# The block inverse's doubling in four half slots instead of two slots, and attention's first row maxima and two of its slots ahead of the recurrence

## The chip, the cores and the metric

The kernel runs on one core of a Trainium2 chip. The metric is the device time of one launch in microseconds (us). Before the change the median of three runs is 3781.65 us (3773.04 to 3784.24). The profiled execution, which all rows below come from, took 3778.69 us.

## The reference

Two layers of a diffusion backbone work on 128 context tokens and 1024 latent tokens of width 1024. In each layer one input projection feeds three groups of heads: a bidirectional recurrence (RWKV-7, 4 heads of 64, two directions), attention over compressed keys (8 heads), and a gated chunk MLP. One output projection joins them, a normalisation follows, then a SwiGLU feed-forward part and a second normalisation. The two groups that matter here are these, cut to their core:

```python
# recurrence, for each direction, each head and each token
s_kk = einsum('hvk,hk->hv', S, -kk_t)
S = S * w_t[None] + s_kk[..., None] * (kk_t * a_t) + v_t[..., None] * k_t
y_t = einsum('hvk,hk->hv', S, r_t)
# attention, for each head and block of queries
s = q_nope @ k_nope.T + q_rope @ k_rope.T
o = softmax(s * MLA_SCALE) @ v
```

All arithmetic is fp32 in its result; the kernel makes an fp32 product of three products of rounded halves (lines L119 to L121, high by high, high by low, low by high).

## The kernel before, in words

The recurrence is computed in blocks of 64 tokens: within a block the tokens depend on each other through a triangular matrix, whose inverse is needed, and between blocks a state `S` is handed on. There are nine segments of 128 tokens (`segs`: the context, then eight of latent tokens), each with both directions. For a segment, `rw_operands` loads the columns `zin` and `szin` (L994, L996), multiplies them out into `AR` and `BK` (DVE L1032 to L1035, POOL L1031 and L1038, ACT L1016 to L1021), makes the triangular matrices `M1` on PE (L1052), and hands over to `rw_solve`. That routine writes the matrices to DRAM and reads back their 16 x 16 diagonal blocks `Db`, 64 of them, one in each partition. DVE inverts these blocks by doubling: from 1 x 1 to 2, 4, 8 and 16 (`for s in (2, 4, 8)` after a first copy, L1093). Each doubling is two products (`x` = 0 and 1), each of them some multiplications (L1113) and a sum (L1114). The result `Xb` goes, with its transpose (L1118), to DRAM as `xbd` (L1120) and comes back as `xz` in four loads (L1125), spread to the shape that PE wants. `rw_double` builds the 64 x 64 inverses from it on PE (L1140 to L1164), and `rw_scan` carries the state: `R` (L1182), `UV` (L1188 to L1191), the sums `St` and `S` on DVE (L1208, L1209), the outputs `Y`. For finished blocks of tokens `rw_post` normalises, gates and stores them in six steps (L1243 to L1279); its working tile `po_y` has two buffers.

Attention is a generator (`other`). For one head and 512 queries it computes the row maxima of a later unit (PE L735 with DVE L740 and L746, then through PE L753 and ACT L754 as one more row of the queries `qT`), the scores (L119 to L121), the exponentials (ACT L762, into `P` with four buffers), the sums over them (POOL L847), and the products with the values (PE L867). At a unit's end come the sums' reciprocal (DVE L777) and the store of the result (ACT's queue, L782). The next unit's keys, queries and values are loaded from ACT's queue as well (L786, L729, L791). One yield of the generator is half a group: two key tiles' scores with up to two row maxima, or the products of the group before.

In the stretch around the change the order of all five engines is written by hand (`manual_schedule`). A turn `i` of the loop has six slots; in slot `k` the function `slot(first, work)` emits attention's next half (scores and maxima), then the list `first`, then attention's other half (products, reciprocal), then the list `work`. The lists hold one step each of `rw_scan` of segment `i`, of `flow[i + 1]` to `flow[i + 3]` (the operands and solves of later segments) and of `rw_post`. Turn -2 is the first, so that segment 0's scan has its inverse; after the loop attention alone goes on with the last posts, and then the generator's rest up to the output projection, whose weights (`wr<-in_w_out_dram`, L309) and rows (`wr<-yd`, L1311) are loaded there. Engines run their own lists in order and wait for each other by semaphores; SP issues the loads and stores that the code puts on `nc.sync`.

Of the kernel before, what the change touches and what calls it, by code (L numbers as in the profile page):

```python
# [8 lines left out]
F32 = mybir.dt.float32  # L9
# [69 lines left out]
class Net:  # L79
# [637 lines left out]
    def mla(self, l, ap):  # L717
# [81 lines left out]
        q_tiles = {x: [self.t(ap, [NQR, 2, nq], f"qT{x}{i}", F32R) for i in range(n)] for x, nq, n in (("", 512, 3), ("c", 128, 2))}  # L799
        k_tiles = [self.t(ap, [NQR, 2, NK], f"kT{i}", F32R) for i in range(2)]  # L800
        for n, t in enumerate([k_tiles[0], q_tiles[""][0], q_tiles[""][1], q_tiles["c"][0], k_tiles[1], q_tiles[""][2], q_tiles["c"][1]]):
            (nc.gpsimd if n % 2 else nc.vector).memset(t[96:128].bitcast(F32), 0.0)
        for t in k_tiles:
            nc.vector.memset(t[96:97, 0].bitcast(F32), 1.0)
            nc.sync.dma_start(t[64:96].bitcast(F32), self.krd)

        units = [(h, q) for h in range(8) for q in ([0], [T_LAT, 512])]
# [82 lines left out]

    def rwkv(self, l, rp, other):
        nc = self.nc
        g2 = self.t(rp, [128, 256], "rg2")
        nc.gpsimd.dma_start(g2, self.I["rw_g2"][l])
        hv = self.t(rp, [128, 4], "rhv")
        nc.vector.tensor_scalar(hv[:, 0:2], self.v(l, "rw_ka", 0, 2), -1.0, None, op0=ALU.mult)
        nc.vector.tensor_scalar(hv[:, 2:4], self.v(l, "rw_ka", 0, 2), -1.0, 1.0, op0=ALU.mult, op1=ALU.add)

        brk = self.t(rp, [128, 2, 128], "brk")
        for ct in range(2):  # L900
            nc.vector.tensor_scalar(brk[:, ct], self.bones, self.v(l, "rw_rk", ct), None, op0=ALU.mult)

        Q = self.t(rp, [128, 8, 64], "Q")
        nc.gpsimd.memset(Q, 0.0)

        Xb = self.t(rp, [64, 2, 256], "Xb")
        nc.gpsimd.memset(Xb[:, 0], 0.0)
        nc.gpsimd.memset(Xb[:, 0, 0:256:17], 1.0)

        sl = self.t(rp, [64, 2, 4, 64], "so")  # L910
        for d in range(2):
            nc.gpsimd.dma_start(sl[:, d], self.I["state_rwkv"][0, l, d].rearrange("h v k -> v h k"))
        p = self.psum("rc")
        for ct in range(2):
            for d in range(2):
                nc.tensor.transpose(p[:, 64 * (2 * ct + d):64 * (2 * ct + d) + 64], sl[:, d, 2 * ct:2 * ct + 2].rearrange("p a b -> p (a b)"), self.ident[0:64, 0:64])
        S_lat = self.t(rp, [128, 2, 2, 64], "S", bufs=3)
        nc.vector.tensor_copy(S_lat.rearrange("p c u v -> p (c u v)"), p[:, 0:256])
        state = {True: None, False: S_lat}
        Y = self.t(rp, [128, NT, 2, 128], "Y")  # L920

        segs = [(T_LAT, 0, True)] + [(128 * i, T_CTX + 128 * i, False) for i in range(8)]
        n = len(segs)
        kept = [{} for _ in segs]
        flow = [self.rw_operands(segs[i], rp, hv, Q, Xb, self.xbd[i % 4], kept[i]) for i in range(n)]

        def turn(g):
            return lambda: next(g, None)  # L930

        def slot(first, work):

            next(other, None)
            for f in first:
                f()
            next(other, None)
            for f in work:
                f()
        def end_of_context():  # L940
            p = self.psum("rc")
            for d in range(2):
                for ct in range(2):
                    nc.tensor.transpose(p[0:64, 128 * (2 * d + ct):128 * (2 * d + ct) + 128], state[True][:, ct, d, :], self.ident)
            so = self.t(rp, [64, 512], "so")
            nc.vector.tensor_copy(so, p[0:64])
            nc.sync.dma_start(self.O["o_state"][0, l].rearrange("d h v k -> v (d h) k"), so.rearrange("p (a k) -> p a k", k=64))
        for _ in range(6):
            next(flow[0])
        next(other)  # L950

        E = mybir.EngineType
        with self.tc.manual_schedule(engines={E.PE, E.DVE, E.Activation, E.Pool, E.SP}):
            post, posts = [], []
            for i in range(-2, n):
                scan = self.rw_scan(segs[i], rp, Y, state, **kept[i]) if i >= 0 else iter(())
                ends = [turn(p) for p in posts]
                posts = [self.rw_post(l, b, rp, Y, g2, brk) for b in post]
                post = []
                for k in range(6):  # L960
                    first, work = [turn(p) for p in posts], [turn(scan)]
                    if 0 <= i + 2 < n:
                        work.append(turn(flow[i + 2]))
                    if 0 <= i + 3 < n:
                        (first if k == 2 else work).append(turn(flow[i + 3]))
                    if 0 <= i + 1 < n and k != 1:
                        (first if k > 1 else work).append(turn(flow[i + 1]))
                    if (i, k) == (1, 2):
                        first.insert(0, end_of_context)
                    slot(first, work + (ends if k == 0 else []))  # L970
                if i == 0:
                    post.append(8)
                if i >= 5:
                    post += [8 - i, i - 1]
            ends = [turn(p) for p in posts]
            posts = [self.rw_post(l, b, rp, Y, g2, brk) for b in post]
            for k in range(7):
                slot([], [turn(p) for p in posts] + (ends if k == 0 else []))
# [92 lines left out]
    def rw_solve(self, rp, M1, Xb, xd, kept):  # L1071

        nc = self.nc
        rows = (slice(0, 64), slice(64, 128))

        diag = lambda a: a.rearrange("g j (b r) -> (g j b) r", b=4)[:, 0:1024].rearrange("q (s t) -> q s t", t=64)[:, :, 0:16]
        full = lambda a: a[:, 0:4096].rearrange("j (s t) -> s j t", t=64)
        ltd = self.t(self.dram, [2, 8, 4160], "ltd", bufs=2)  # L1080
        for g in range(2):
            nc.sync.dma_start(full(ltd[g]), M1[rows[g], 1 - g, :, :, 0:64].rearrange("p c u t -> p (c u) t"))
        yield
        Db = self.t(rp, [64, 16, 16], "Db", bufs=2)
        nc.sync.dma_start(Db, diag(ltd))
        yield

        X, D = Xb[:, 0], Db.rearrange("p a b -> p (a b)")

        def at(a, o, *dims):  # L1090

            return bass.AP(a.tensor, a.offset + o, [a.ap[0], *([x, y] for x, y in dims)])
        nc.vector.tensor_copy(at(X, 16, (34, 8)), at(D, 1, (34, 8)))  # L1093
        for s in (2, 4, 8):
            b = 8 // s
            q = self.t(rp, [64, 64], "Xq")
            for x in range(2):
                pr = self.t(rp, [64, 512], "pr_x")

                if x == 0:  # L1100
                    l, m = (D, s, 34 * s, 1, 0, 16), (X, 0, 34 * s, 0, 1, 16)
                    o = q[:, 0:s * s * b]
                else:
                    l, m = (X, 17 * s, 34 * s, 16, 0, 1), (q, 0, s * s, 0, 1, s)
                    o = at(X, 16 * s, (34 * s, b), (16, s), (1, s))

                def part(a, o, sb, si, sj, sk):

                    if s == 2:
                        return [at(a, o + j * sj, (sb, b), (si, s), (sk, s)) for j in range(s)]  # L1110
                    return [at(a, o + i * sb, (si, s), (sj, s), (sk, s)) for i in range(b)]
                for p_, l_, m_ in zip(part(pr, 0, s ** 3, s * s, s, 1), part(*l), part(*m)):
                    nc.vector.tensor_tensor(p_, l_, m_, op=ALU.mult)  # L1113
                nc.vector.tensor_reduce(o, pr[:, 0:s ** 3 * b].rearrange("p (a k) -> p a k", k=s), axis=AX.X, op=ALU.add)  # L1114
            if s == 4:
                yield
        Xs, Xt = (Xb[:, x].rearrange("p (a b) -> p a b", a=16) for x in range(2))
        nc.vector.tensor_copy(Xt, Xs.rearrange("p a b -> p b a"))  # L1118
        for x, y in enumerate((Xs, Xt)):
            nc.sync.dma_start(diag(xd[x]), y)  # L1120
        yield
        xz = kept["xz"] = self.t(rp, [128, 2, 8, 64], "xz", bufs=3)
        for x in range(2):
            for g in range(2):
                nc.sync.dma_start(xz[rows[g], x], full(xd[x, g]))  # L1125
        yield
# [99 lines left out]
    def rw_post(self, l, b, rp, Y, g2, brk):  # L1226
# [13 lines left out]
        def tmp(tag):  # L1240
            return self.t(rp, [128, 2, 128], tag, bufs=2)
        p = bank()
        nc.tensor.matmul(p, self.bones, y, start=True, stop=True)  # L1243
        yc = tmp("po_y")
        nc.vector.scalar_tensor_tensor(yc, p, -1.0 / 64, y, op0=ALU.mult, op1=ALU.add)
        sq = tmp("po_t")
        nc.scalar.activation(sq, yc, AF.Square)
# [414 lines left out]
```

## Time and profile before

| | |
|---|---|
| median of three runs | 3781.65 us |
| profiled execution | 3778.69 us, its span 3776.9 us |
| mean granted TensorE clock | 0.957 of full speed |
| PE busy in the span | 3519.4 us (93%) |
| DVE, ACT, POOL busy | 1883.6 (50%), 1098.7 (29%), 1372.8 us (36%) |
| recurrence beside attention, layer 0 | 366 to 785 us |
| the same, layer 1 | 2236 to 2665 us |

The span is almost filled by PE, and what isn't lies for a good part in the two stretches of the last rows. A clock of 0.5 in a stretch is the lower of TensorE's two levels (1.2 GHz), 1.0 the higher (2.4 GHz).

### The profile page before, as it was taken

Reading aid. Unit: us, or ns where it says so; the run is one execution under the profiler, and the core shown is the slowest. Engines: PE = TensorE matmul, PEld = TensorE weight load, DVE = VectorE, ACT = ScalarE, POOL = GpSimd, SP = SyncE. Lnnn points to the kernel's source line nnn. Section 1 sums busy time; section 2 is a strip of 40 time slices with the busy share of each in tenths; the row PEclk is TensorE's granted clock in tenths of the full one; section 3 lists DMA queues with packets and bytes.
Section 4 is the critical chain, followed back from the end, with each engine's and each line's share of the span. In section 5 each row is a group of like instructions: output and inputs, shape, how many; then the busy total and the mean of one; then the engine's idle time right before and its main releaser. Section 6 shows DMA issues by size and latency. Waiting matters only on the chain.

```text
span 3776.9 us, 61399 instructions
## 1 busy us (share of the span) xinstructions
PE 3519.4 (93%) x25199; PEld 3048.4 (81%) x25199; DVE 1883.6 (50%) x3076; ACT 1098.7 (29%) x2156; POOL 1372.8 (36%) x1223
## 2 busy tenths in 40 slices
PE   8998788888999999999999988888998999999996
PEld 6888566666988888988988885666778999999995
DVE  3545665655733333333455465566559333333356
ACT  3443444423421111111144434343333311111111
POOL 2322656644511111111543237556445111111145
PEclk9999788999999999999999998899999999999998
DMA  7566545434332222221325565444343111111122
GB/s 288 158 220 164 114 100 104 96 77 149 107 107 78 90 79 78 67 67 56 107 103 143 192 147 109 99 97 88 78 159 107 51 45 45 39 40 45 45 84 78
DMA packets 466137, 387.13 MB, mean 102 GB/s; under 512 B 171148, under 2 KB 398856, under 8 KB 464640
## 3 DMA queue, kind: packets, MB, share of 16 engines
q1 hardware_dynamic: 372608, 249.12, 23.7%
q10 hardware_dynamic: 87424, 118.42, 10.4%
q0 software_dynamic: 5824, 15.66, 1.3%
q8 instruction: 198, 3.24, 0.4%
q14 instruction: 83, 0.68, 0.1%
HBM read 280.10 MB, written 103.02 MB: 101 GB/s over the span
## 4 chain that ended last, share of the span: by engine, by line
PE 74%; DVE 12%; DMA 6%; issue 2%; ACT 2%; POOL 1%; SPq 1%; ACTq 0%; POOLq 0%; DVEq 0%
PE b L119 19%; PE b L121 18%; PE b L120 18%; PE b L867 3%; DVE pr_x L1113 2%; PE b L355 2%; PE b L242 2%; DMA xz<-xbd 2%; DVE mx L740 1%; PE b L735 1%; PE b L406 1%; DVE hyl L126 1%; PE b L1140 1%; DMA zin<-zd 1%; DVE rc L777 1%
## 5 line engine op out<-in xcount | busy, mean ns | idle before, releaser
L121 PE MATMUL b<-hyh,w 128*128 128x384 f32 x2544 | 858.8, 338 | 1.4 <-DVE w L319 1.4
L119 PE MATMUL b<-hyh,w 128*128 128x384 f32 x2448 | 823.1, 336 | 0.0
L120 PE MATMUL b<-hyl,w 128*128 128x384 f32 x2448 | 821.9, 336 | 0.0
L319 POOL TENSOR_TENSOR w<-wr,w 128x2048 fp32r<-128x2048 f32 x64 | 296.9, 4640 | 1189.2 <-ACT w L316 989.0
L121 PEld LDWEIGHTS b<-hyh,w 128*128 128x128 f32 x2544 | 479.0, 188 | 26.3 <-issue 23.9
L119 PEld LDWEIGHTS b<-hyh,w 128*128 128x128 f32 x2448 | 460.1, 188 | 20.8 <-issue 19.4
L120 PEld LDWEIGHTS b<-hyl,w 128*128 128x128 f32 x2448 | 460.1, 188 | 9.7 <-issue 8.3
L1406 DVE TENSOR_TENSOR fs<-fs,b 128x384 f32<-128x384 f32 x132 | 72.9, 553 | 627.1 <-PE b L121 623.0
L847 POOL TENSOR_TENSOR acc<-acc,P 128x512 f32<-128x512 f32 x224 | 297.1, 1326 | 179.4 <-ACT P L762 169.9
L316 ACT CAST w<-wr 128x2048 fp32r<-128x2048 f32 (+2 forms) x86 | 161.2, 1874 | 583.8 <-PE b L120 511.9
L120 PE MATMUL b<-w,hidh 128*128 128x512 f32 x756 | 299.5, 396 | 0.0
L121 PE MATMUL b<-w,hidl 128*128 128x512 f32 x756 | 299.4, 396 | 0.0
L119 PE MATMUL b<-w,hidh 128*128 128x512 f32 x756 | 298.3, 396 | 0.0
L126 DVE TENSOR_TENSOR hidl<-fs,hidh 128x384 fp32r<-128x384 f32 x126 | 230.6, 1831 | 81.5 <-ACT hidh L125 79.5
L1420 DVE TENSOR_TENSOR acc<-acc,b 128x512 f32<-128x512 f32 x288 | 191.5, 684 | 139.0 <-PE b L121 139.0
L762 ACT ACTIVATE P<-b 128x512 f32<-128x512 f32 x288 | 169.7, 600 | 207.8 <-PE b L121 176.8
L740 DVE TENSOR_REDUCE mx<-b 128x1 f32<-128x512 f32 x256 | 169.0, 682 | 120.2 <-PE b L735 119.4
L867 PE MATMUL b<-P,vt 128*64 128x256 f32 x1152 | 180.1, 432 | 3.9 <-ACT P L762 3.2
L119 PE MATMUL b<-w,hyh 128*128 128x256 f32 x576 | 167.0, 292 | 16.9 <-ACT hyh L125 5.4
L125 ACT CAST hidh<-fs 128x384 fp32r<-128x384 f32 x126 | 64.4, 512 | 396.4 <-DVE fs L1406 396.4
L119 PE MATMUL b<-qT,kT 128*128 128x512 f32 x288 | 138.4, 480 | 38.3 <-DVE mx L740 30.0
L1405 ACT ACTIVATE fs<-b 128x384 f32<-128x384 f32 x132 | 64.8, 493 | 372.5 <-PE b L121 362.2
(437 smaller groups left out, 6953.1 us busy)
## 6 DMA issues: line engine op xcount, KB each, us to landing
wr<-in_ffn_w_in_dram SPq DMA_DIRECT2D x88, 512.0 KB, 4.7
fx<-in_ada_w_dram SPq DMA_DIRECT2D x28, 1024.0 KB, 5.1
wr<-in_ffn_w_out_dram SPq DMA_DIRECT2D x22, 1024.0 KB, 4.8
wr<-in_ada_w_dram SPq DMA_DIRECT2D x20, 1024.0 KB, 8.8
qT<-qd ACTq DMA_DIRECT2D x32, 448.0 KB, 6.3
zin<-zd SPq DMA_DIRECT2D x36, 384.0 KB, 5.3
xres<-x ACTq DMA_DIRECT2D x27, 512.0 KB, 3.6
wr<-in_w_in_dram SPq DMA_DIRECT2D x12, 1024.0 KB, 6.2
```

The source lines that it names most:

```text
L119: mm(out, ah, bh, start=(i == 0), stop=False)
L120: mm(out, ah, bl, start=False, stop=False)
L121: mm(out, al, bh, start=False, stop=(i == n - 1))
L126: (lo_eng or self.nc.vector).tensor_tensor(lo, src, hi.bitcast(F32), op=ALU.subtract)
L242: nc.tensor.matmul(p[32 * jj:32 * jj + 32, :], self.sc[:, 2 * jj + e, :], w[:, 2 * j + e, :], start=(e == 0), stop=(e == 1), tile_position ...
L316: self.nc.scalar.copy(hi, r)
L319: (eng or self.nc.gpsimd).tensor_tensor(lo[:, s], r[:, s], hi[:, s].bitcast(F32), op=ALU.subtract)
L740: nc.vector.tensor_reduce(mx[:, i, c:c + 1], p, axis=AX.X, op=ALU.max)
L762: nc.scalar.activation(P[:, 0:nq], p[:, 0:nq], AF.Exp, scale=MLA_SCALE)
L847: nc.gpsimd.tensor_tensor(acc, Ps[0] if k == 1 else acc, P, op=ALU.add)
L867: nc.tensor.matmul(po[0][64 * i:64 * i + 64, 0:256], vt[:, k], Ps[k][:, 256 * i:256 * i + 256], start=(k == 0), stop=(k == 9))
L1420: nc.vector.tensor_tensor(acc[i][:, w], acc[i][:, w], p, op=ALU.add)
```

## The change

- `kT`, `qT` and `qTc` are cleared, and the rows of ones set, by POOL alone; before, DVE made six of these nine fills.
- `rwkv` takes attention's first step, which is the first unit's row maxima (and the second unit's loads), as its first act, ahead of its own set-up (`rg2`, `hv`, `brk`, the states); before, that step came after the first six steps of `flow[0]`.
- Two slots with attention alone precede the loop's first turn.
- `rw_solve` yields after the second product of s = 2, after that of s = 4, after the first product of s = 8, and after the copy and the stores; before, it yielded after s = 4 and after the stores. So the doubling takes four half slots (`first` and `work` of slots 4 and 5) instead of the `work` of slots 4 and 5.
- The steps of `flow[i + 1]` go into `first` in every slot but slot 1; before, in slots 0 they stood in `work`. These steps include the four `xz` loads.
- `po_y` has four buffers instead of two.

```diff
@@ -799,9 +799,9 @@
         q_tiles = {x: [self.t(ap, [NQR, 2, nq], f"qT{x}{i}", F32R) for i in range(n)] for x, nq, n in (("", 512, 3), ("c", 128, 2))}
         k_tiles = [self.t(ap, [NQR, 2, NK], f"kT{i}", F32R) for i in range(2)]
         for n, t in enumerate([k_tiles[0], q_tiles[""][0], q_tiles[""][1], q_tiles["c"][0], k_tiles[1], q_tiles[""][2], q_tiles["c"][1]]):
-            (nc.gpsimd if n % 2 else nc.vector).memset(t[96:128].bitcast(F32), 0.0)
+            nc.gpsimd.memset(t[96:128].bitcast(F32), 0.0)
         for t in k_tiles:
-            nc.vector.memset(t[96:97, 0].bitcast(F32), 1.0)
+            nc.gpsimd.memset(t[96:97, 0].bitcast(F32), 1.0)
             nc.sync.dma_start(t[64:96].bitcast(F32), self.krd)
 
         units = [(h, q) for h in range(8) for q in ([0], [T_LAT, 512])]
@@ -890,6 +890,7 @@
 
     def rwkv(self, l, rp, other):
         nc = self.nc
+        next(other)
         g2 = self.t(rp, [128, 256], "rg2")
         nc.gpsimd.dma_start(g2, self.I["rw_g2"][l])
         hv = self.t(rp, [128, 4], "rhv")
@@ -947,11 +948,12 @@
             nc.sync.dma_start(self.O["o_state"][0, l].rearrange("d h v k -> v (d h) k"), so.rearrange("p (a k) -> p a k", k=64))
         for _ in range(6):
             next(flow[0])
-        next(other)
 
         E = mybir.EngineType
         with self.tc.manual_schedule(engines={E.PE, E.DVE, E.Activation, E.Pool, E.SP}):
             post, posts = [], []
+            for _ in range(2):
+                slot([], [])
             for i in range(-2, n):
                 scan = self.rw_scan(segs[i], rp, Y, state, **kept[i]) if i >= 0 else iter(())
                 ends = [turn(p) for p in posts]
@@ -960,11 +962,13 @@
                 for k in range(6):
                     first, work = [turn(p) for p in posts], [turn(scan)]
                     if 0 <= i + 2 < n:
-                        work.append(turn(flow[i + 2]))
+
+                        for part in (first, work) if k > 3 else (first if k == 3 else work,):
+                            part.append(turn(flow[i + 2]))
                     if 0 <= i + 3 < n:
                         (first if k == 2 else work).append(turn(flow[i + 3]))
                     if 0 <= i + 1 < n and k != 1:
-                        (first if k > 1 else work).append(turn(flow[i + 1]))
+                        first.append(turn(flow[i + 1]))
                     if (i, k) == (1, 2):
                         first.insert(0, end_of_context)
                     slot(first, work + (ends if k == 0 else []))
@@ -1112,8 +1116,8 @@
                 for p_, l_, m_ in zip(part(pr, 0, s ** 3, s * s, s, 1), part(*l), part(*m)):
                     nc.vector.tensor_tensor(p_, l_, m_, op=ALU.mult)
                 nc.vector.tensor_reduce(o, pr[:, 0:s ** 3 * b].rearrange("p (a k) -> p a k", k=s), axis=AX.X, op=ALU.add)
-            if s == 4:
-                yield
+                if s == 8 and x == 0 or s < 8 and x == 1:
+                    yield
         Xs, Xt = (Xb[:, x].rearrange("p (a b) -> p a b", a=16) for x in range(2))
         nc.vector.tensor_copy(Xt, Xs.rearrange("p a b -> p b a"))
         for x, y in enumerate((Xs, Xt)):
@@ -1241,7 +1245,7 @@
             return self.t(rp, [128, 2, 128], tag, bufs=2)
         p = bank()
         nc.tensor.matmul(p, self.bones, y, start=True, stop=True)
-        yc = tmp("po_y")
+        yc = self.t(rp, [128, 2, 128], "po_y", bufs=4)
         nc.vector.scalar_tensor_tensor(yc, p, -1.0 / 64, y, op0=ALU.mult, op1=ALU.add)
         sq = tmp("po_t")
         nc.scalar.activation(sq, yc, AF.Square)
```

SP's list around the stores of the first inverse (`xbd`), the loads of it (`xz`) and the next segment's columns (`zin`, `szin`); line numbers of the changed kernel are three or four higher here. Before:

```order
L1120 DMA xbd_462_2859<-Xb_3666 64x16x16 x2
L994 DMA szin_4173<-sd_70 128x4x128
L996 DMA zin_4175<-zd_69 128x6x128
L994 DMA szin_4177<-sd_70 128x4x128
L996 DMA zin_4179<-zd_69 128x6x128
L1125 DMA xz_4181<-xbd_462_2859 64x8x64 x4
L1003 DMA UV_4172<-vtd_71 64x256 x4
```

After:

```order
L1124 DMA xbd_462_2859<-Xb_3734 64x16x16 x2
L1129 DMA xz_4207<-xbd_462_2859 64x8x64 x4
L998 DMA szin_4231<-sd_70 128x4x128
L1000 DMA zin_4233<-zd_69 128x6x128
L998 DMA szin_4235<-sd_70 128x4x128
L1000 DMA zin_4237<-zd_69 128x6x128
L1007 DMA UV_4230<-vtd_71 64x256 x4
```

The `xz` loads have moved past the four column loads.

DVE's list at the start of the third inverse (`Xb`, from `Db`). Before:

```order
L777 RECIPROCAL rc_4918<-b_843_4915 128x256
L1093 COPY Xb_3666<-Db_4860 64x8
L1113 TENSOR_TENSOR pr_x_4934<-Db_4860,Xb_3666 64x8x2 x2
L1114 TENSOR_REDUCE Xq_4933<-pr_x_4934 64x16
L1113 TENSOR_TENSOR pr_x_4938<-Xb_3666,Xq_4933 64x8x2 x2
L1114 TENSOR_REDUCE Xb_3666<-pr_x_4938 64x4x2x2
L1113 TENSOR_TENSOR pr_x_4943<-Db_4860,Xb_3666 64x64 x2
L1114 TENSOR_REDUCE Xq_4942<-pr_x_4943 64x32
L1113 TENSOR_TENSOR pr_x_4947<-Xb_3666,Xq_4942 64x64 x2
L1114 TENSOR_REDUCE Xb_3666<-pr_x_4947 64x2x4x4
L1032 TENSOR_TENSOR AR_852_4951<-zin_4608,PB_809_4694 128x2x2x64
L1033 TENSOR_TENSOR pr_k_4699<-pr_k_4699,zin_4608 128x256
```

After:

```order
L740 TENSOR_REDUCE mx_4660<-b_851_4934 128x1
L740 TENSOR_REDUCE mx_4660<-b_854_4944 128x1
L746 TENSOR_REDUCE eye_3656<-b_855_4947 128x1
L1097 COPY Xb_3734<-Db_4857 64x8
L1117 TENSOR_TENSOR pr_x_4952<-Db_4857,Xb_3734 64x8x2 x2
L1118 TENSOR_REDUCE Xq_4951<-pr_x_4952 64x16
L1117 TENSOR_TENSOR pr_x_4956<-Xb_3734,Xq_4951 64x8x2 x2
L1118 TENSOR_REDUCE Xb_3734<-pr_x_4956 64x4x2x2
L1117 TENSOR_TENSOR pr_x_4996<-Db_4857,Xb_3734 64x64 x2
L1118 TENSOR_REDUCE Xq_4995<-pr_x_4996 64x32
L1117 TENSOR_TENSOR pr_x_5000<-Xb_3734,Xq_4995 64x64 x2
L1118 TENSOR_REDUCE Xb_3734<-pr_x_5000 64x2x4x4
```

The copy and the four rows of s = 2 were behind the reciprocal of attention's sums, and the reciprocal isn't in this place any more, since attention runs two slots ahead. Between s = 2 and s = 4 lies attention's half slot, which has no DVE work of its own here.

DVE's list at the end of the same inverse, with the scan's `St`, `S` and `Y`. Before:

```order
L740 TENSOR_REDUCE mx_4774<-b_856_4966 128x1
L740 TENSOR_REDUCE mx_4774<-b_859_4976 128x1
L1208 TENSOR_TENSOR St_5030<-b_861_5004,S_4742 128x256
L1209 TENSOR_TENSOR S_5029<-St_5030,EP_3693 128x256
L1221 TENSOR_TENSOR Y_3679<-Y_3679,b_861_5004 128x2x64
L1222 TENSOR_TENSOR Y_3679<-Y_3679,b_861_5004 128x2x64
L1113 TENSOR_TENSOR pr_x_5036<-Db_4860,Xb_3666 64x512
L1114 TENSOR_REDUCE Xq_5035<-pr_x_5036 64x64
L1113 TENSOR_TENSOR pr_x_5039<-Xb_3666,Xq_5035 64x512
L1114 TENSOR_REDUCE Xb_3666<-pr_x_5039 64x8x8
L1118 COPY Xb_3666<-Xb_3666 64x256
```

After:

```order
L740 TENSOR_REDUCE mx_4660<-b_869_5019 128x1
L740 TENSOR_REDUCE mx_4660<-b_872_5028 128x1
L1117 TENSOR_TENSOR pr_x_5035<-Db_4857,Xb_3734 64x512
L1118 TENSOR_REDUCE Xq_5034<-pr_x_5035 64x64
L1212 TENSOR_TENSOR St_5087<-b_877_5061,S_4808 128x256
L1213 TENSOR_TENSOR S_5086<-St_5087,EP_3761 128x256
L1225 TENSOR_TENSOR Y_3747<-Y_3747,b_877_5061 128x2x64
L1226 TENSOR_TENSOR Y_3747<-Y_3747,b_877_5061 128x2x64
L1117 TENSOR_TENSOR pr_x_5092<-Xb_3734,Xq_5034 64x512
L1118 TENSOR_REDUCE Xb_3734<-pr_x_5092 64x8x8
L1122 COPY Xb_3734<-Xb_3734 64x256
```

The first product of s = 8 (one multiplication, one sum) now stands ahead of `St` and `S`, the second one behind `Y` as before.

## Rows read from the trace of the kernel before

**Rows 1.** Windows: length, busy us (count) of PE, PEld, DVE, ACT, POOL, PEclk:

```profile
366.00:785.00 419.00, 343.39 (x4160) 258.15 (x4159) 255.31 (x480) 161.85 (x370) 241.63 (x263) 0.86 0.49 105
...
521.00:525.00 4.00, 4.00 (x44) 3.87 (x44) 1.63 (x4) 2.91 (x9) 2.59 (x3) 0.50 1.03 189
...
2236.00:2665.00 429.00, 354.53 (x4269) 269.72 (x4267) 258.58 (x491) 162.79 (x372) 242.04 (x263) 0.88 0.47 103
```

**Rows 2.** Waits of PE, 366 to 785: engine, line, releaser: total us, times, longest:

```profile
PE b L119 <- DVE mx L740: 14.3, 8, 4.4
PE b L735 <- ACT P L762: 12.7, 5, 5.9
PE b L1140 <- DMA xz<-xbd: 9.9, 7, 3.5
PE b L735 <- DVE mx L740: 9.4, 5, 3.4
PE b L1252 <- ACT po_t L1247: 6.7, 1, 6.7
...
PE b L1162 <- DVE po_y L1277: 3.8, 1, 3.8
```

**Rows 3.** Waits of PE in the second layer, 2236 to 2665:

```profile
PE b L119 <- DVE mx L740: 15.8, 9, 4.4
PE b L1140 <- DMA xz<-xbd: 12.7, 5, 5.5
PE b L735 <- ACT P L762: 11.3, 5, 6.0
```

**Rows 4.** Timeline of DVE from 488: start, us, engine, line, [idle before]:

```profile
491.49 1.76 DVE L777 RECIPROCAL rc<-b 128x256 f32<-128x256 f32 x1 [3.54 <-PE b L775]
...
493.30 0.82 DVE L1113 TENSOR_TENSOR pr_x<-Db,Xb 64x16 f32<-64x16 f32 x2
...
495.22 1.20 DVE L1113 TENSOR_TENSOR pr_x<-Db,Xb 64x64 f32<-64x64 f32 x2
...
498.10 0.65 DVE L1032 TENSOR_TENSOR AR<-zin,PB 128x256 f32<-128x256 f32 x1
...
502.56 1.69 DVE L1113 TENSOR_TENSOR pr_x<-Db,Xb 64x512 f32<-64x512 f32 x1
```

**Rows 5.** DMA issues, 366 to 785: count, KB each, us to landing:

```profile
xz<-xbd SPq DMA_DIRECT2D x36, 128.0 KB, 5.4
...
xbd<-Xb SPq DMA_DIRECT2D x18, 64.0 KB, 2.6
```

**Rows 6.** Line L1125, the xz loads of 366 to 785:

```profile
DMA to landing us min/median/max: 4.5/5.4/7.2
```

**Rows 7.** Timeline of SP's queue from 415 (same columns):

```profile
426.44 0.62 SPq L994 DMA_DIRECT2D szin<-sd  x1
...
428.84 3.40 SPq L1125 DMA_DIRECT2D xz<-xbd  x4
```

**Rows 8.** Timeline of ACT and its queue from 429:

```profile
435.19 1.85 ACTq L782 DMA_DIRECT2D yd<-o  x2
```

**Rows 9.** Timeline of ACT and its queue from 511:

```profile
519.37 0.59 ACTq L729 DMA_DIRECT2D qT<-qd  x1
```

**Rows 10.** Timeline of DVE from 768:

```profile
782.75 0.76 DVE L1245 SCALAR_TENSOR_TENSOR po_y<-b,Y 128x256 f32<-128x256 f32 x2 [8.70 <-DMA yd<-po_y]
```

**Rows 11.** Timeline of ACT from 366:

```profile
381.46 1.28 ACT L1016 ACT_TABLE_LOAD   x1 [14.11 <-DMA szin<-sd]
```

**Rows 12.** Timeline of PE from 864, the loop's tail:

```profile
870.70 0.40 PE L119 MATMUL b<-qT,kT 128*128 128x512 f32 x1
...
871.48 1.08 PE L867 MATMUL b<-P,vt 128*64 128x256 f32 x8
...
887.12 0.55 PE L119 MATMUL b<-w,hyh 128*128 128x256 f32 x1 [3.90 <-POOL acc L847]
```

**Rows 13.** Timeline of SP's queue from 866:

```profile
879.76 15.62 SPq L309 DMA_DIRECT2D wr<-in_w_out_dram  x3
```

## The prediction

> **What bounds the kernel now.** The page comes first: PE is busy for 93% of the span, so that time can only come from stretches in which PE stands still or runs at the lower clock. Two windows hold the whole of the recurrence with its attention, one for each layer [rows 1]. PE is busy 343.4 of 419 us in the first and 354.5 of 429 in the second, so 75.6 and 74.5 us are idle, and the granted clock is 0.86 and 0.88. A clock of 0.5 for a share x and 1.0 for the rest gives 0.86 at x = 0.28; half of 0.28 x 343.4 is 48 us that the work took longer than at the higher level, in the second layer 0.24 / 2 x 354.5 = 43 us. The lower level follows idle time: behind the stand that ends with ACT's late load issue at 519.37 [rows 9] PE works all 4.00 us of 521 to 525 at 0.50 [rows 1]. So an idle microsecond drags about 0.6 us behind it (48 / 75.6, 43 / 74.5).
>
> Next is the list of PE's waits [rows 2, 3]. Four releasers make most of it: DVE's row maxima (14.3 + 9.4 us, 15.8 in the first line of layer 1), ACT's exponentials (12.7 and 11.3), the `xz` loads (9.9 and 12.7), and the last posts (6.7 + 3.8). The timelines tell what stands behind each. In DVE's [rows 4] it waits 3.54 us for PE, makes attention's reciprocal, and only then turns to the doubling: s = 2 from 493.30 to 495.22, 1.9 us; s = 4 to 498.10, 2.9 us; the operands; the maxima, which PE needs; from 502.56 on s = 8. ACT's exponentials are late because its queue stood still in issuing a load or a store: the store at 435.19 goes out only when an `xz` load has come in, the query load at 519.37 when a column load has [rows 8, 9]. I read this from the coincidence of issue and landing.
>
> **The change part by part**, for each layer.
>
> *The `xz` loads ahead of the column loads.* On SP the four column loads begin at 426.44 and hold the first `xz` issue to 428.84, 2.4 us [rows 7]. But the stores that `xz` reads back land 2.6 us after their issue [rows 5], so the first issue can move by only about 1 us of this; the four issues, 3.40 us, should close up, and landing should go from the median of 5.4 towards the fastest, 4.5 [rows 5, 6]. I take 2 us earlier. PE's waits of that kind are 7 with a mean of 1.4 and 5 with a mean of 2.5 us; what lies beyond 2 us in the longest (3.5, 5.5) stays. That is -7.5 us, bounds 0 and -12.7. The price is that the columns come about 3 us later; `PB` and `AR` are due two slots on, and I price this with the scan below.
>
> The Trainium skill ("DMA: Bandwidth & Descriptors", section "Queues, rings and completion order") says that a queue's descriptors are consumed in the order of its ring on each DMA engine. The spread of 4.5 to 7.2 us for one size of load fits that. By this rule the moved loads gain just what the column loads lose, which is the mechanism of my second rival below; no figure of the page enters the sum.
>
> *ACT's queue.* With another order of issues ACT will stand behind other landings. One of the two long stands per layer (5.9 and the one before 521) should shorten, another may appear. -3 us, bounds 0 and -11.3.
>
> *Doubling in four half slots.* DVE's instructions are the same, so nothing is gained but where it was idle: s = 2 can now go into time like the 3.54 us ahead of the reciprocal, and the burst ahead of the maxima loses up to 1.9 us. Nine inverses per layer: with all of it -17, with none 0. I take half, 1 us each, -9: the row maxima waits (23.7 us) have room for it, but attention is two slots ahead of before against the recurrence, and not every inverse will find an idle stretch there.
>
> *The first product of s = 8 ahead of the scan's `St` and `S`.* It is a multiplication of 1.69 us [rows 4] with its sum. The next `R` on PE waits for `S`; attention's half slot covers most of that. With cover it costs 0, without 1.7 us in each of nine inverses, +15. With the later columns I take +3.
>
> *Four `po_y` buffers.* DVE waits 8.70 us for the stores of two posts before it may write the next `po_y` [rows 10], and PE waits 6.7 and 3.8 us in consequence [rows 2]. The buffer wait goes entirely. Late next is the `xz` of the last inverse, which PE needs in the same place; no row shows that wait, so I take half of each, -3 and -2, -5 together; bounds -1 and -10.5.
>
> *Fills on POOL, first maxima early, two slots alone.* PE begins after `szin` lands at 381.46 and ACT's chain behind it [rows 11]; the column loads wait for the last stores of the projection, and DVE's fills stand in one list with the copies that these stores take. POOL's first work on the operands needs `szin` too, so its nine fills have the time before 381.46 as cover; without it they would add what DVE saves. ACT makes both directions' operands ahead of the first query row now, which gives back part. -1.5, bounds +1 and -4. The two slots themselves are work that is moved and not less.
>
> *The tail.* What attention does early is missing at the end. After the last post the list of PE has 15 wide score products and 8 value products fewer than before. Three of the one kind take 0.78 us (870.70 to 871.48) and eight of the other 1.08 [rows 12], so 3.9 + 1.1 = 5 us less work stands beside the loads of the output projection. PE waits 3.90 us there already, and the weights' issue ends the queue's idle time at 879.76 [rows 12, 13]. I take +4, bounds 0 and +6.
>
> The sum of idle time is -7.5 - 3 - 9 + 3 - 5 - 1.5 + 4 = -19 us. Of the -21.5 us that lie in the loop, 0.6 us each would come back by the clock if every shortened gap vanished; many only shrink, so I take half, 0.3 x 21.5 = 6.5. That is -25.5 us a layer, -51 for two. The profiled execution took 3778.7 us, which becomes 3727.7; the median of the runs is 3 us above it, so 3731. With the loop's terms at half or at one and a half times their size the change is about -23 or -80: 3700 to 3760 is the forecast's own range.
>
> **Rivals.**
>
> *Larger gain.* Both long ACT stands go, the `xz` waits go entirely, and s = 2 always finds idle time: -12 - 10 - 12 - 7 - 2 + 4 = -39 us idle, and with most gaps gone the full 0.6 on 41 us, -25: -64 a layer, 3654. For it: each wait has one named releaser that the change touches. Against it: ACT's stands depend on whichever load is in flight, and there are more loads than the change moves.
>
> *No change.* DVE's work between one pair of maxima and the next is what it was, the columns lose what `xz` gains, and ACT stands behind the columns instead: only `po_y` and the start stay (-6.5), and the tail (+4) and the scan (+3) take them back: 3782. For it: the same totals on each engine, and DVE's row of waits, which the idle 3.54 us can only partly relieve.
>
> *Slower.* The product of s = 8 ahead of `S` delays the state, and with it `R`, `UV` and every later scan of a chain that attention's products can't cover: +15, `po_y` -5, `xz` -4 since PE then waits for the scan instead, together +6, with the clock (x 1.6) +10, and tail and start +6: +16 a layer, 3813. It decides from about 0.6 us per inverse on, where 9 x 0.6 = 5.4 against -9, times 1.6, with +6 is zero. Against it: attention's half slot lies between `S` and the next `R`, several matmuls long.
>
> **How the numbers follow.** Forecast 0.55, larger gain 0.13, no change 0.20, slower 0.12. What a measurement of this kernel can't tell from no change is within 0.3%, 11 us. The forecast and the larger gain are faster, and of "no change" 0.03 falls out on each side. From the slower rival 0.02 may end within. So faster 0.71, same 0.16, slower 0.13. The range leaves out most of the larger gain and the upper half of the slower rival: 3675 to 3795; the likeliest case alone is 3700 to 3760.
>
> **What would show it.** Right: PE's waits for `xz` fall to some 4 us a layer; its waits for row maxima by a third; DVE's wait for the `po_y` stores is gone and the wait of L1252's successor shorter than 4 us; idle time in the two windows falls from 75 to about 55 us and the granted clock rises to about 0.88 and 0.90. The wait ahead of the output projection's first product grows by some 4 us. Wrong: if the windows' busy time and clock are unchanged, DVE's bursts only moved; if PE waits for `S` or ACT's `R` in the loop, the slower rival has it; if the ACT waits vanish altogether with the `xz` waits, the gain is the larger one.

## The result, and the profile after

The changed kernel takes 3739.61 us (median of four runs, 3733.92 to 3744.40) against 3782.94 us in the same comparison: a ratio of 0.9895, interval 0.9876 to 0.9914. That is 43 us less by the medians and 40 by the ratio. The profiled execution took 3735.45 us, its span 3733.7.

Windows of both kernels from the projection's end to the end of the output projection, one for each layer (length; busy us and count of PE, PEld, DVE, ACT, POOL; PE's clock). Before:

```profile
361.00:1020.00 659.00, 563.86 (x6088) 446.64 (x6088) 403.82 (x730) 249.26 (x538) 363.69 (x369) 0.89 0.45 109
...
2243.00:2902.00 659.00, 567.43 (x6137) 452.69 (x6136) 413.30 (x726) 248.41 (x536) 363.89 (x356) 0.90 0.42 104
```

After:

```profile
361.00:996.00 635.00, 545.87 (x6086) 437.73 (x6086) 398.55 (x722) 249.13 (x538) 373.04 (x376) 0.93 0.46 113
...
2220.00:2862.00 642.00, 562.39 (x6135) 450.62 (x6134) 413.97 (x728) 248.14 (x534) 366.90 (x356) 0.91 0.43 107
```

Layer 0 is 24 us shorter, layer 1 17 us; that is 41 of the 43 us between the two profiled executions. PE's busy time fell by 18.0 and 5.0 us at the same work, by the clock; its idle time fell from 95.1 to 89.1 and from 91.6 to 79.6 us. So the clock gave back more (23 us) than the idle time itself (18 us).

PE's waits after, first the recurrence of layer 0, then of layer 1; they answer to [rows 2, 3], in slightly longer windows (line numbers are four higher where the code moved):

```profile
PE b L735 <- DVE mx L740: 11.9, 4, 4.1
PE b L873 <- DVE mx L740: 8.5, 2, 4.2
PE b L735 <- ACT P L762: 8.0, 6, 2.3
PE b L735 <- DVE rc L777: 7.5, 4, 4.1
PE b L119 <- DVE mx L740: 6.7, 5, 1.8
PE b L1150 <- ACT BT L1069: 6.1, 2, 5.4
...
PE b L1144 <- DMA xz<-xbd: 0.8, 2, 0.6
...
PE b L1166 <- DVE po_y L1281: 0.4, 1, 0.4
```

```profile
PE b L735 <- ACT P L762: 10.6, 7, 2.9
PE b L735 <- DVE mx L740: 10.3, 5, 3.2
PE b L873 <- DVE mx L740: 8.5, 2, 4.2
PE b L1150 <- ACT BT L1069: 8.2, 2, 7.4
PE b L735 <- DVE rc L777: 5.0, 4, 2.1
PE b L119 <- DVE mx L740: 4.9, 6, 1.8
...
PE b L1144 <- DMA xz<-xbd: 1.4, 3, 0.7
```

The `xz` waits are all but gone (9.9 to 0.8, 12.7 to 1.4), and so are those of the last posts (6.7 and 3.8 us in layer 0 to 0.4). DVE's part is not: maxima and reciprocal, 34.6 us in layer 0 and 28.7 in layer 1 (28.8 and 31.0 before). The loads of `xz` also land sooner; layer 0, line L1129, against 4.5/5.4/7.2 in [rows 6]:

```profile
DMA to landing us min/median/max: 2.8/3.8/5.2
```

New is L1150, which waits for ACT's copy `BT`. Its longest wait in layer 0, and ACT's timeline before it:

```profile
448.92 0.43 PE L1150 MATMUL b<-Q,xz 64*64 64x32 f32 x4 [5.38 <-ACT BT L1069]
```

```profile
442.61 0.42 ACT L1020 ACTIVATE PB<-szin 128x256 f32<-128x256 f32 x1 [3.74 <-DMA szin<-sd]
...
446.48 0.42 ACT L1020 ACTIVATE PB<-szin 128x256 f32<-128x256 f32 x1 [2.38 <-DMA szin<-sd]
...
448.29 1.06 ACT L1069 COPY BT<-b 128x512 f32<-128x512 f32 x2
```

ACT stands for the column loads, 3.74 and 2.38 us, and the copy is queued behind their exponentials. The columns behind `xz` alone don't cost this. Among the runs below only those with early `xz`, the two slots and a doubling in more than two pieces have these waits above 3 us a layer (4.5 to 8.7). With the same order of loads and no split (e1) they are 1.9 and 1.0 us: there ACT, by the profile, stands for the same two loads, 4.12 and 3.53 us, but the first stand comes ahead of one of attention's exponentials, where PE waits 3.83 us, and 1.21 are left at this place. What moves the stand to `BT` isn't shown.

### The profile page after: what moved, and what is told of

Its sections match the earlier page's. It is cut to its first block, busy times and chain, and to the rows that moved or that the text cites. A ratio compares the mean times of both kernels' runs of the same rounds, so it can differ in the third digit from the quotient of the medians.

```text
span 3733.7 us, 61460 instructions
## 1 busy us (share of the span) xinstructions
PE 3496.2 (94%) x25199; PEld 3038.1 (81%) x25199; DVE 1869.6 (50%) x3064; ACT 1098.2 (29%) x2156; POOL 1391.5 (37%) x1235
## 4 chain that ended last, share of the span: by engine, by line
PE 73%; DVE 12%; DMA 6%; issue 3%; ACT 3%; POOL 2%; SPq 1%; ACTq 0%; POOLq 0%; DVEq 0%
PE b L119 19%; PE b L121 19%; PE b L120 19%; PE b L867 2%; PE b L355 2%; PE b L242 2%; DVE pr_x L1117 2%; DMA szin<-sd 1%; DVE hyl L126 1%; PE b L735 1%; DVE mx L740 1%; PE b L406 1%; PE b L1056 1%; DMA wr<-in_w_out_dram 1%; DMA xz<-xbd 1%
## 5 line engine op out<-in xcount | busy, mean ns | idle before, releaser
L735 PE MATMUL b<-kT,qT 128*128 128x512 f32 (+1 forms) x384 | 124.1, 382 | 52.8 <-DVE mx L740 22.3
```

Of the source, the lines that this page charges most:

```text
L735: nc.tensor.matmul(p[:, 0:n], qT[0][:, 128 * i:128 * i + 128], kT[0][:, k0:k0 + n], start=True, stop=True)
```

## The experiments

Each ratio is to the kernel before, timed beside it on the same chip. The changed kernel wasn't timed beside these runs, so differences from it are given by medians and by ratios where they disagree. The first four runs take one part out of the changed kernel.

**Without the split** (e1): the slot list and the yields as before.

```diff
-                        for part in (first, work) if k > 3 else (first if k == 3 else work,):
-                            part.append(turn(flow[i + 2]))
+                        work.append(turn(flow[i + 2]))
...
-                if s == 8 and x == 0 or s < 8 and x == 1:
-                    yield
+            if s == 4:
+                yield
```

> The changed kernel, but with the doubling in two slots as before. Theory A (the prediction's): the four half slots relieve the bursts ahead of the row maxima by 9 us a layer, some 12 with the clock, so this kernel is 15 to 25 us slower than the changed one, about 3760. Theory B: DVE's work between one pair of maxima and the next is the same, and the changed kernel's waits for DVE (34.6 and 28.7 us a layer against 28.8 and 31.0) show that nothing was gained: within 8 us of the changed kernel, 3732 to 3748.

Measured 3726.47 us, 0.9851 (0.9837 to 0.9864): faster than the changed kernel. In this company the split costs 13 us by the medians, 17 by the ratios (0.0044 of 3783). Neither theory held. PE's waits for DVE in layer 1 of this run:

```profile
PE b L735 <- DVE mx L740: 17.9, 5, 5.5
PE b L119 <- DVE mx L740: 9.0, 7, 3.5
...
PE b L873 <- DVE mx L740: 7.6, 2, 3.8
...
PE b L735 <- DVE rc L777: 1.7, 3, 1.1
...
PE b L1148 <- ACT BT L1067: 1.0, 1, 1.0
```

Maxima and reciprocal are 36.2 us here, 7.5 more than in the changed kernel (in layer 0 35.2, 0.6 more). So the split does relieve them; what it loses elsewhere is more. The row in which it loses most is the wait for `BT`, 14.3 us in the two layers of the changed kernel and 2.9 here. In the stretches of both layers together PE is idle for 6 us less here, and busy for 7 us less at the same work.

**Without the two slots** (e2):

```diff
-        next(other)
         g2 = self.t(rp, [128, 256], "rg2")
...
+        next(other)
...
-            for _ in range(2):
-                slot([], [])
```

> The changed kernel, but with attention's first maxima behind the recurrence's first steps and without the two slots of attention alone, as before. Theory A: the two slots are moved work that the tail misses, 4 us a layer, and the start gains 1.5: this kernel is about 5 us faster than the changed one, 3735. Theory B: the shift by two slots changes which of attention's steps meet the doubling, and a good part of the gain is that: this kernel is 10 us or more slower, above 3750.

3732.22 us, 0.9860 (0.9844 to 0.9876): theory A's sign, more than its size (7 us by the medians, 13 by the ratios).

**Without the early `xz`** (e3):

```diff
-                        first.append(turn(flow[i + 1]))
+                        (first if k > 1 else work).append(turn(flow[i + 1]))
```

> The changed kernel, but with the steps of flow[i + 1] in slot 0 back in the list work, so that the xz loads stand behind the column loads. Theory A: PE's waits for xz come back (0.8 and 1.4 us in the changed kernel, 9.9 and 12.7 before) and bring the lower clock with them, while the waits behind ACT's copy of BT (6.1 and 8.2 us) go: about 10 us slower than the changed kernel, 3750. Theory B: what the xz loads gain the column loads lose: within 5 us.

3759.00 us, 0.9940 (0.9927 to 0.9953): theory A at twice its size. The loads' order is worth 17 (by the ratios) to 19 us here, and the columns don't take it back.

**Without the fills on POOL** (e4):

```diff
-            nc.gpsimd.memset(t[96:128].bitcast(F32), 0.0)
+            (nc.gpsimd if n % 2 else nc.vector).memset(t[96:128].bitcast(F32), 0.0)
...
-            nc.gpsimd.memset(t[96:97, 0].bitcast(F32), 1.0)
+            nc.vector.memset(t[96:97, 0].bitcast(F32), 1.0)
```

> The changed kernel, but with the fills of kT and qT split between DVE and POOL as before. Theory A: POOL's ten microseconds of fills in one row hold ACT's loads (7.33 us idle before L131, released by POOL's kT) and PE's last products of the projection (5.7 us), so that this kernel is 3 to 8 us faster, 3732 to 3737. Theory B (the prediction's): fills on DVE delay the copies of the projection as much: within 3 us or slower.

3733.23 us, 0.9867 (0.9852 to 0.9881): theory A's size, though the interval touches the changed kernel's. Its cause doesn't hold. In ACT's timeline of the changed kernel the copy behind the loads of `kT` and `qT` stands for a fill:

```profile
366.24 0.37 ACT L131 COPY zc<-b 128x256 f32<-128x256 f32 x1 [7.33 <-POOL kT L804]
```

With the fills on DVE (e4) ACT stands as long just ahead of the same copy, for DVE's copy `zc`:

```profile
368.85 0.38 ACT L559 ACTIVATE kk<-b 128x256 f32<-128x256 f32 x1 [7.09 <-DVE zc L133]
```

Counted from POOL's L708 ahead of the fills, ACT's L131 begins after 20.6 us in the changed kernel and after 21.0 here, and PE's products for `M1` after 51.2 and 50.8 us. So at most half a microsecond of the gain lies at layer 0's start; where the rest comes from isn't shown.

The next four add parts to the kernel before: **the buffers** (e5, `po_y` with `bufs=4`), **the early `xz`** (e6, the reverse of e3's edit), **the split** (e7, the reverse of e1's), **buffers and early `xz`** (e8).

> The kernel before with four po_y buffers and nothing else. Theory A: the two waits (6.7 and 3.8 us a layer) are gone in the changed kernel (0.6 us left), and with the clock this part alone gives 15 to 30 us: 3754 to 3769. Theory B (the prediction's size): half of the waits is replaced by the next wait, for xz, so the part gives some 10 to 13 us: about 3772.

3775.78 us, 0.9981 (0.9969 to 0.9993): 7 us, less than either size. Layer 0's waits show what is late next:

```profile
PE b L1140 <- DMA xz<-xbd: 12.1, 8, 5.0
...
PE b L1162 <- DVE po_y L1277: 3.7, 1, 3.7
```

The wait for the posts' L1247 is gone, that for `xz` has grown from 9.9 to 12.1 us (in layer 1 from 12.7 to 16.9), and L1162 still waits 3.7.

> The kernel before with the early xz loads and nothing else. Theory A: the gain seen when this part was undone in the changed kernel (19 us) belongs to this part by itself: about 3765, with PE's xz waits down from 9.9 and 12.7 to under 3 us a layer. Theory B: it needs the shift of the two slots to pay; here ACT stands longer for the column loads: within 6 us of 3784.

3755.66 us, 0.9935 (0.9919 to 0.9952): theory A, 25 us by this part alone. PE's waits for `xz` are gone in layer 0 and 1.7 us in layer 1.

> The kernel before with the doubling in four half slots and nothing else. Theory A (from the run without the split): the split costs some 10 us by itself, about 3794, because the first product of s = 8 and the second one still both stand ahead of the next maxima and the inverse is out later. Theory B (the prediction): it gains 9 us of idle time a layer, about 3760. Theory C: it costs only beside the early xz loads: within 5 us of 3784.

3779.57 us, 0.9992 (0.9977 to 1.0008): theory C's value (its condition fails below, since beside the early `xz` in e11 the split costs nothing). Layer 0's waits show that this isn't for want of an effect:

```profile
PE b L735 <- ACT P L762: 16.0, 7, 6.8
...
PE b L119 <- DVE mx L740: 7.5, 5, 4.4
PE b L735 <- DVE rc L777: 6.9, 3, 3.9
...
PE b L735 <- DVE mx L740: 6.2, 5, 2.1
...
PE b L1181 <- DVE Y L1223: 3.6, 2, 1.8
```

Before, the two maxima rows were 14.3 + 9.4 us [rows 2]; here they are 13.7 together, 10.0 less. But the reciprocal makes PE wait 6.9 us (1.9 before), the scan waits 3.6 us for DVE's `Y`, and PE waits 3.3 us more for ACT's exponentials.

> The kernel before with four po_y buffers and the early xz loads, without the split, the two slots and the fills on POOL. Theory A: what was undone one by one (13, 7 and 6 us) adds up, and this kernel is 20 to 26 us faster than the changed one: 3714 to 3720. Theory B: the three overlap, since without the two slots the split meets other steps: 3726 or more.

3747.87 us, 0.9912 (0.9897 to 0.9928). Buffers and early `xz` add up (7 + 25 against 33 us); the other parts' removal doesn't, so theory B.

Of the last four, e9 and e11 combine the other three parts differently, with buffers and early `xz` on throughout (the fills alone were not run). e9 is e1 with e4's edit; e10 is the changed kernel with s = 8 behind the scan:

```diff
-                if s == 8 and x == 0 or s < 8 and x == 1:
-                    yield
+            if s < 8:
+                yield
+            if s == 4:
+                yield
```

> Four po_y buffers, the early xz loads, the first maxima early and the two slots, but neither the split nor the fills on POOL. Theory A: the fills on POOL cost 6 us here too, and the two slots gain by shifting attention against the recurrence: about 3720, 6 us under the run without the split alone and 28 under the run with buffers and xz only. Theory B: the fills matter only together with the split: 3724 to 3730.

3729.60 us, 0.9860 (0.9843 to 0.9878): theory B. Against e8 the first maxima early and the two slots gain 20 us by the ratios, 18 by the medians. PE's largest row of waits for ACT's exponentials in layer 1, e8 and then e9:

```profile
PE b L735 <- ACT P L762: 17.6, 8, 8.3
```

```profile
PE b L735 <- ACT P L762: 7.9, 3, 3.2
```

In layer 0 it fell from 14.1 to 8.3 us, and the last posts' wait at L1162 fell from 3.7 to 0.4 in each layer. Maxima and reciprocal rose, from 31.2 and 29.1 to 36.7 and 35.5 us. In the stretches of both layers together PE is idle for 8 us less and busy for 18 us less.

> The changed kernel with s = 8 whole in the last half slot, behind the scan's St and S; s = 2 and s = 4 stay in half slots of their own and the fourth is empty. Theory A: what the split costs beside the two slots is the first product of s = 8 ahead of the reciprocal and of S (PE's waits for the reciprocal are 7.5 and 5.0 us a layer in the changed kernel, 1.6 and 1.7 without the split): this kernel is 8 to 14 us faster than the changed one, 3726 to 3732. Theory B: the cost comes from s = 4 being later, or from what the split does to the loads: within 5 us of 3740.

3737.17 us, 0.9882 (0.9869 to 0.9896) against 0.9895: theory B. The first product of s = 8 is not what the split costs. The waits for `BT` are still there (4.5 and 8.2 us).

> Four po_y buffers, the early xz loads and the split, but neither the two slots nor the fills on POOL. Theory A: the split and the two slots both relieve the same bursts of DVE ahead of the row maxima, each alone is worth some 20 us beside the early xz loads, and they do not add: 3722 to 3732 against 3748 without the split. Theory B: the split is worth nothing in any company, and the run without slots owes its time to the fills on POOL: 3744 or more.

3742.04 us, 0.9885 (0.9866 to 0.9904): between the theories, nearer to B. The split is worth 10 us here by the ratios and 6 by the medians, and the intervals overlap; it is worth 0 alone and loses 13 to 17 beside slots and fills.

| split | slots | fills | ratio to before | run |
|---|---|---|---|---|
| - | - | - | 0.9912 | e8 |
| yes | - | - | 0.9885 | e11 |
| - | yes | - | 0.9860 | e9 |
| - | yes | yes | 0.9851 | e1 |
| yes | - | yes | 0.9860 | e2 |
| yes | yes | - | 0.9867 | e4 |
| yes | yes | yes | 0.9895 | changed |

Over e8 the slots (with the first maxima early, which no run separates from them) gain 20 us and the split may gain 10; the fills add nothing that can be told from zero beside the slots alone (e9 to e1). Beside the other two each of the three loses, by the ratios 17 us (split), 13 (slots) and 11 (fills). All three together are worth 6 us over e8, which can't be told from zero, so that buffers and early `xz`, with 33 us, carry the change. The version without the split (e1, 0.9851) beats both kernels, about 56 us under the one before.

**Without POOL's sums** (e12), to see what stretches DVE's multiplications; attention's sums are set to one:

```diff
-                    if k:
-                        nc.gpsimd.tensor_tensor(acc, Ps[0] if k == 1 else acc, P, op=ALU.add)
+                    if k == 1:
+                        nc.gpsimd.memset(acc, 1.0)
```

> The changed kernel with POOL's sums over the exponentials left out (the sums are set to one, so attention's output is not the reference's): 224 additions of 1.3 us less on POOL. Theory A: DVE's multiplications with both inputs in SBUF are slowed by POOL's work beside them: the doubling's 64 x 512 products fall from a mean of 1.12 and 1.27 us to about 1.0, its 64 x 64 ones from 0.34 and 0.49 to about 0.27, S from 0.70 to 0.45, and PE's waits for row maxima fall by a third or more; operations with one input in PSUM keep their 0.42. Theory B: the spread of these durations has to do with something else: they stay within 10%.

DVE's groups in layer 0 (busy us, mean ns | idle before), the changed kernel and this one:

```profile
L1037 DVE TENSOR_TENSOR pr_k<-pr_k,zin 128x256 f32<-128x256 f32 x18 | 14.9, 829 | 0.0
L1039 DVE TENSOR_TENSOR BK<-szin,pr_i 128x256 f32<-128x256 f32 x18 | 14.9, 827 | 0.6 <-POOL szin L1026 0.6
...
L1117 DVE TENSOR_TENSOR pr_x<-Xb,Xq 64x512 f32<-64x512 f32 x9 | 11.4, 1269 | 0.1
...
L1117 DVE TENSOR_TENSOR pr_x<-Db,Xb 64x512 f32<-64x512 f32 x9 | 10.1, 1118 | 0.0
L1213 DVE TENSOR_TENSOR S<-St,EP 128x256 f32<-128x256 f32 x14 | 9.7, 695 | 0.5
...
L1146 DVE TENSOR_TENSOR Q<-b,cst 128x256 f32<-128x256 f32 x9 | 3.8, 425 | 13.8 <-PE b L1144 13.8
```

```profile
L1037 DVE TENSOR_TENSOR pr_k<-pr_k,zin 128x256 f32<-128x256 f32 x18 | 10.7, 594 | 0.0
L1117 DVE TENSOR_TENSOR pr_x<-Xb,Xq 64x512 f32<-64x512 f32 x9 | 10.3, 1145 | 0.1
...
L1117 DVE TENSOR_TENSOR pr_x<-Db,Xb 64x512 f32<-64x512 f32 x9 | 9.8, 1089 | 0.0
...
L1039 DVE TENSOR_TENSOR BK<-szin,pr_i 128x256 f32<-128x256 f32 x18 | 9.0, 500 | 0.6 <-POOL szin L1026 0.6
...
L1213 DVE TENSOR_TENSOR S<-St,EP 128x256 f32<-128x256 f32 x16 | 7.8, 487 | 0.5
...
L1146 DVE TENSOR_TENSOR Q<-b,cst 128x256 f32<-128x256 f32 x9 | 3.8, 425 | 15.3 <-PE b L1144 15.3
```

Theory A for all but the 64 x 512 products, of which one fell by a tenth and the other by 3%. L1146, which has one input in PSUM, kept its 425 ns. PE's waits for maxima and reciprocal fell from 34.6 and 28.7 to 10.4 and 11.4 us. All 256 additions are out (the 224 expected are one of their two forms), with 32 fills on POOL in their place. The run took 3671.93 us (0.972, 0.9697 to 0.9743), but less work is in it, and how much of the 68 us is DVE's alone isn't shown.

## Why the prediction was right, step by step

The time lay in the range and in the forecast's own range: 51 us were forecast, 43 came. The mechanism of its two shown gains, the loads' order and the buffers, was right; that the sum of the rest came out near is luck, since its terms were off both ways.

- *`xz` ahead of the columns*, -7.5 us of waits a layer: undersized. -9.1 and -11.3 came. The first issue moved by about the 1 us that was taken (the column loads held it for 2.4 us; after, it comes 1.26 us behind the stores' issue). The four issues didn't close up at that place (3.32 us against 3.40), but the landing went from 5.4 to 3.8 us in the median, past the 4.5 that was hoped for. It is the largest gain measured: 25 of the 43 us by itself (e6).
- *Columns later and S behind s = 8*, +3 together: 6.1 and 8.2 us at L1150, where ACT stands for the columns, undersized, and only beside the split and the slots. The scan's part was small: 1.3 us at L1184 (`Y`) in the trace after, and e10 shows no cost that can be told from zero.
- *ACT's queue*, -3: 12.7 to 8.0 us and 11.3 to 10.6, about right in size, but not by the mechanism that was forecast. The other order of loads alone leaves 12.3 and 16.3 us (e6); with the slots and without it (e3) there are 11.2 and 10.6, and e8 to e9 the slots take 5.8 and 9.7 us away.
- *The two slots*, put at nothing ("work that is moved and not less"): this step failed. With the first maxima early they gain 20 us beside buffers and early `xz` (e8 to e9), and beside split and fills they cost 13. Which steps of attention and recurrence meet differently by them isn't shown.
- *Doubling in four half slots*, -9: this step failed too. It took the maxima's waits (23.7 us in layer 0) as a place where DVE's idle time could be put, and was to show in the waits for maxima falling by a third; with L873 they went from 26.9 to 27.1 us and from 29.1 to 23.7. The split alone takes 10 us off them (e7), but PE then waits for the reciprocal, the scan and ACT instead, and the time stays. In the changed kernel maxima and reciprocal are 34.6 and 28.7 us instead of 28.8 and 31.0: the slots raised them (e9), and the split took only 0.6 and 7.5 us back (e1), less than the waits for `BT` that came with it. One of these waits in the changed kernel, DVE first and PE behind it:

```profile
507.32 0.68 DVE L1118 TENSOR_REDUCE Xq<-pr_x 64x64 f32<-64x512 f32 x1
...
508.36 1.49 DVE L1213 TENSOR_TENSOR S<-St,EP 128x256 f32<-128x256 f32 x1
...
510.17 1.05 DVE L1117 TENSOR_TENSOR pr_x<-Xb,Xq 64x512 f32<-64x512 f32 x1
...
512.26 1.27 DVE L740 TENSOR_REDUCE mx<-b 128x1 f32<-128x512 f32 x2
```

```profile
512.99 0.56 PE L873 MATMUL b<-accc,vt 128*64 128x128 f32 x2 [4.25 <-DVE mx L740]
```

  Between two pairs of maxima DVE has s = 8's first product with its sum, `St`, `S` and `Y`, the second product and the copy; PE's L873 wants a bank that the maxima free, and waits 4.25 us (without the split, e1, its longest wait is 3.8). The instructions between the maxima are the same as before; the rival "no change" had that right for this part.
- *Buffers*, -5 a layer, with the clock some 13 in all: oversized, 7 us alone and 9 beside the early `xz` (e6 to e8). The wait of 6.7 us went. The one of 3.8 at L1162 was not the buffers' (3.7 in e5 and in e8); it goes with the slots (0.4 in e9). Alone, `xz` was late next, as forecast (2.2 and 4.2 us more).
- *Start*, -1.5: not borne out, as far as the fills go. I priced them as what DVE saves, with POOL's free time as cover; the starts of the changed kernel and of e4 agree within half a microsecond, since ACT stands 7.33 us for POOL's fills in the one and 7.09 us for DVE's copy in the other. Undone they give 6 us by the medians (e4), though nothing without the split (e9 and e1); the cause of the 6 us stays open.
- *Tail*, +4: confirmed. Waits at the output projection's start, before and after:

```profile
PE b L119 <- POOL acc L847: 3.9, 1, 3.9
PE b L867 <- ACT P L762: 2.8, 1, 2.8
```

```profile
PE b L119 <- ACT w L316: 10.8, 2, 6.9
```

  The waits of that stretch sum to 12 us before and 16 after; in layer 1 PE's idle time there goes from 8.7 to 13.4 us.
- *The clock*, -6.5 a layer: undersized. Idle time fell by 6 and 12 us, and busy time by 18 and 5, so that an idle microsecond brought 1.3 us of clock and not 0.3. In layer 0 the clock went from 0.89 to 0.93 with 6 us less idle time in sum, so it seems to count which gaps vanish; no run tries that by itself.

So the idle time was overestimated (19 a layer forecast, 9 on average), the clock underestimated (6.5 against 11.5), and by luck the two errors mostly cancel. That the split and the slots interact is shown by the table; which coincidence of steps makes each cell of it is not, and stays open.

## What to carry to other kernels

When loads share a queue, put the one that the critical engine waits for ahead of those due two slots later: it was the largest gain here, and it came in both kernels (25 us added to the one before, 17 to 19 in the changed one). A burst on one engine that is cut in pieces moves the wait to what stands behind the pieces; price the two or three instructions that are queued there. Parts of a schedule change should be tried one by one and in pairs: of five parts here two add up, and the other three gain up to 20 us or lose up to 17 depending on each other.

## What the runs showed of the hardware that was not expected

DVE operations with both inputs in SBUF take longer when POOL works beside them: with the 256 additions of POOL taken out, `pr_k` (L1037) fell from 829 to 594 ns, `BK` (L1039) from 827 to 500, `S` (L1213) from 695 to 487, while a product with one input in PSUM stayed at 425 (e12). The Trainium skill says as much of the two engines' shared SBUF interfaces ("GPSIMD Engine Reference", section "Key points"), for DVE instructions with two SBUF inputs; the runs here put a price on it, in the groups shown from 3% (1118 against 1089 ns) to 65% (827 against 500) on top of the shorter duration. POOL still has other work beside them in e12 (216 us in layer 0's stretch, 376 with the additions). A copy with its one input in SBUF fell as well (L1122, 569 to 430 ns); DVE's reductions of 64 x 512 from SBUF stayed at 678.
